# A macaron encoder layer on one core: where tiles start in their partition, once multiples of 32 bytes, now multiples of 512

## Chip, core and metric

The kernel runs on one core of a Trainium2 chip, in one launch. The metric is the device time of an execution in microseconds (us). Engines are named as in the profile: PE is TensorE (PEld its weight loads), DVE VectorE, ACT ScalarE, POOL GpSimd, SP the engine that issues most transfers.

## What is computed

One layer, 512 tokens of 1024 channels, all in float32 (the two SwiGLU blocks have 2816 hidden channels):

```python
h = h + 0.5 * swiglu(rms_norm(h, ffn1_norm), ffn1_w_gate, ffn1_w_up, ffn1_w_down)
u = rms_norm(h, mix_norm) @ w_in            # q 512 | k 128 | v 128 | pool channels 512
a = window_attention(rope(q), rope(k), v, sink_logits)   # +-128 tokens, 8 heads, 2 kv heads
p = multiscale_pool(pc, pool_w, pool_scale)              # windows 2, 4, 8, 16
h = h + concat([a, p]) @ w_out
h = h + 0.5 * swiglu(rms_norm(h, ffn2_norm), ffn2_w_gate, ffn2_w_up, ffn2_w_down)
out = rms_norm(h, final_norm)
```

## The kernel before

Channels lie on the 128 partitions, tokens along the row. Every large product runs in the type float32r, on operands split into a high and a low half (`xh` and `xl` for an activation, `wh` and `wl` for a weight). `mm3` (lines 99 to 102) makes a product of two split operands from three matmuls: high with high, high with low, low with high. Each has a stationary operand of 128 by 128 (`lhsT`) and a moving operand of 128 by 512 (`rhs`). In the names that the profile gives, `ps<-xl,wh` is a product that reads the tiles `xl` and `wh`.

The layer runs in this order, and PE has work nearly throughout:

- `gate_up` of the first SwiGLU. Six output banks are first filled together over the eight channel tiles `k`, then one hidden tile `f` after another. The weights are stationary, `xh` and `xl` move.
- `down` of the first SwiGLU: weights stationary, the hidden values `a1h` and `a1l` move.
- The mixing stage: the input projection moves `yh` and `yl`, which reuse the place of `xh` and `xl`. The scores have queries `qq` stationary and keys `kk`, `kl` moving, 256 or 384 columns wide. The weighted sums move `ph` and `pl`. The output projection moves `pdh`, `pdl` (pool half) and `qq` (attention half, which reuses the queries' place).
- `gate_up` of the second SwiGLU, as the first, with `zh` and `zl` in the place of `xh` and `xl`.
- `down` of the second SwiGLU, the other way round: the hidden values `a2h`, `a2l` are stationary and the weights `wh`, `wl` move. Its last four hidden tiles lie in `late`, which takes the place of `h`, and the last two weight units of its stream are split into `w2`, which takes the place of `xl`.

Weights come in units of 0.75 or 1 MB on SP's queue into `raw`; ACT rounds each half into `wh` (line 88), DVE subtracts to give `wl` (line 89). All tiles come from pools (`base`, `wts`, and one pool for each stage). A pool gives each tile the next free place in the partition, in the order in which the tiles are first named, rounded up to 32 bytes. Small tiles (`warm`, `gain`, `sink`, `psc`, `epsb`, `nst`) stand between the large ones, for instance

```python
    warm = base.tile([P, 1], F32, name="warm")
...
    h = base.tile([P, KD, S], F32, name="h", tag="h")
    gain = base.tile([P, 3, KD], F32, name="gain")
```

Of the kernel before, what the change touches and what calls it, by code (L numbers as in the profile page):

```python
# [8 lines left out]
F32 = mybir.dt.float32  # L9
# [4 lines left out]
P = 128  # L14
D = 1024
S = 512
DFF = 2816
KD = D // P
NF = DFF // P
NT = S // P  # L20
HD = 64
NH = 8
# [8 lines left out]
PAD = 8  # L31
# [3 lines left out]
def encoder_layer(ctx: ExitStack, tc: tile.TileContext, xT, w1h, w1gu, w1d, win, wout, w2h, w2gu, w2d,  # L35
# [3 lines left out]
    base = ctx.enter_context(tc.tile_pool(name="base", bufs=1))  # L39
    wts = ctx.enter_context(tc.tile_pool(name="wts", bufs=2))  # L40
    psp = ctx.enter_context(tc.tile_pool(name="psp", bufs=8, space=bass.MemoryType.PSUM))

    def bank():
        return psp.tile([P, S], F32, name="ps", tag="ps")

# [1 line left out]
    units = [(w1h, i) for i in range(KD // 2)] + [(w1gu, i) for i in range(NF - F0)]  # L47
    units += [(w1d, i) for i in range(NF // 2)] + [(win, i) for i in range(5)]
    units += [(wout, i) for i in range(4)] + [(w2h, i) for i in range(KD // 2)]
# [1 line left out]
    stream = {"asked": 0, "raw": None, "ready": []}  # L51
# [15 lines left out]
        return raw, n  # L67

    def split_next():
        """w = hi + lo, each exact in float32r."""  # L70
        i, half = stream["asked"] // 2, stream["asked"] % 2
        if i == len(units):
            return
        if half == 0 and i:
            stream["raw"] = load(i)
        raw, n = stream["raw"]
        src = raw[:, half * n:(half + 1) * n]
        spare = stream.get("spare")
        if spare:
            wh, wl = spare.pop(0)  # L80
        else:
            wh = wts.tile([P, 1024], F32R, name="wh", tag="wh", bufs=4)[:, :n]
            wl = wts.tile([P, 1024], F32R, name="wl", tag="wl", bufs=4)[:, :n]
        m = n // 2 if stream["asked"] == 0 else n
        on_pool = WIN_POOL if units[i][0] is win else WOUT_POOL if units[i][0] is wout else ()
        sub = nc.gpsimd if 2 * units[i][1] + half in on_pool else nc.vector
        for c in range(0, n, m):
            nc.scalar.copy(wh[:, c:c + m], src[:, c:c + m])  # L88
            sub.tensor_tensor(wl[:, c:c + m], src[:, c:c + m], wh[:, c:c + m].bitcast(F32),  # L89
                              op=ALU.subtract)  # L90
        stream["asked"] += 1
        stream["ready"].append((wh, wl))
# [8 lines left out]
        nc.tensor.matmul(ps, lhsT=ah, rhs=bl, start=False, stop=False)  # L101
        nc.tensor.matmul(ps, lhsT=al, rhs=bh, start=False, stop=stop)  # L102

# [1 line left out]
    ones = base.tile([P, P], F32, name="ones")  # L105
    nc.vector.memset(ones, 1.0)
    warm = base.tile([P, 1], F32, name="warm")
    nc.scalar.copy(warm, ones[:, 0:1])
    ps = bank()
    for i in range(WARM):  # L110
        nc.tensor.matmul(ps[:, 0:P], lhsT=ones, rhs=ones, start=True, stop=True)
    h = base.tile([P, KD, S], F32, name="h", tag="h")
    gain = base.tile([P, 3, KD], F32, name="gain")

    def xload(*ks):
        for k in ks:
# [7 lines left out]
    stream["raw"] = load(0, start)  # L124
    early[1] = load(1)
    xload(4, 5, 6, 7)
    sink = base.tile([P, 1, NH], F32, name="sink")
    nc.gpsimd.dma_start(sink[:, 0, :], sinks)
    psc = base.tile([P, 4], F32, name="psc")
    nc.gpsimd.dma_start(psc, pscale)  # L130
    ident = base.tile([P, P], F32, name="ident")
    make_identity(nc, ident)
    epsb = base.tile([P, 1], F32, name="epsb")
    nc.vector.memset(epsb, EPS)

    acc = base.tile([P, S], F32, name="acc")
# [4 lines left out]
    xl = base.tile([P, KD, S], F32R, name="xl", tag="xl")  # L141

    def norm_in(n, k, xh, xl):
        """gain * h, split; the mean square is gathered beside it."""
        g = gain[:, n, k:k + 1]
        nc.scalar.activation(xh[:, k, :], h[:, k, :], AF.Copy, scale=g)
        nc.vector.scalar_tensor_tensor(xl[:, k, :], h[:, k, :], g, xh[:, k, :].bitcast(F32),  # L147
                                       op0=ALU.mult, op1=ALU.subtract)
        if n == 0:
            if k == 0:  # L150
                nc.gpsimd.tensor_tensor(acc, h[:, k, :], h[:, k, :], op=ALU.mult)
                return
            nc.gpsimd.tensor_tensor(rtmp, h[:, k, :], h[:, k, :], op=ALU.mult)
            nc.gpsimd.tensor_tensor(acc, acc, rtmp, op=ALU.add)
        elif k == 0:
            nc.scalar.activation(acc, h[:, k, :], AF.Square)
        else:
            sq = base.tile([P, S], F32, name="sq", tag="u", bufs=2)
            nc.scalar.activation(sq, h[:, k, :], AF.Square)
            nc.gpsimd.tensor_tensor(acc, acc, sq, op=ALU.add)  # L160

    nst = base.tile([P, 3, NT], F32, name="nst")

    def newton(r, v, b):
        """r = 1 / sqrt(v) from b = sqrt(v), with a step of Newton's."""
        nc.vector.reciprocal(r, b)
        nc.vector.tensor_tensor(b, r, r, op=ALU.mult)
        nc.vector.tensor_tensor(b, b, v, op=ALU.mult)
        nc.vector.tensor_scalar(b, b, -0.5, 1.5, op0=ALU.mult, op1=ALU.add)
        nc.vector.tensor_tensor(r, r, b, op=ALU.mult)  # L170

    def norm_sums():
        """Tokens on partitions: 1 / rms, then a diagonal that the next step spreads."""
        ps = bank()
        for t in range(NT):
            nc.tensor.matmul(ps[:, t:t + 1], lhsT=acc[:, t * P:(t + 1) * P], rhs=ones[:, 0:1],
                             start=True, stop=True)
        r, v, b = (nst[:, j, :] for j in range(3))
        nc.scalar.activation(b, ps[:, 0:NT], AF.Sqrt, scale=1.0 / D, bias=epsb)
        nc.vector.tensor_scalar(v, ps[:, 0:NT], 1.0 / D, EPS, op0=ALU.mult, op1=ALU.add)  # L180
        newton(r, v, b)
        for t in range(NT):
            nc.vector.tensor_scalar(rtmp[:, t * P:(t + 1) * P], ident, r[:, t:t + 1], None, op0=ALU.mult)
        return ps
# [2 lines left out]
        nc.tensor.matmul(ps, lhsT=ones, rhs=rtmp, start=True, stop=True)  # L187
        nc.scalar.copy(rstd, ps)

# [1 line left out]
    def gate_up(xh, xl, act, tmp, after_first, before=None, each=None):  # L191
        def glu(f, pg, pu):
            t1 = tmp.tile([P, S], F32, name="t1", tag="t1", bufs=2)
# [43 lines left out]
                each(f)  # L237

    def down(act, tokens_first, finish):
        """Products over DFF in eight banks; `finish(i, bank)` as each is complete."""  # L240
        banks = [bank() for _ in range(8)]

        def one(i, k, wh, wl, last):
# [21 lines left out]
                one(i, k, wh, wl, k == NF - 1)  # L265
            finish(i, banks[i])

    # ======================= FFN 1 =======================
    with tc.tile_pool(name="ffn1", bufs=1) as fp:
        a1h = fp.tile([P, NF, S], F32R, name="a1h")  # L270
        a1l = fp.tile([P, NF, S], F32R, name="a1l")
# [1 line left out]
                before=lambda k: norm_in(0, k, xh, xl))  # L273
# [6 lines left out]

        down(lambda f: (a1h[:, f, :], a1l[:, f, :]), False, finish1)

    # ======================= mixing =======================
    def weave(main, fill):
        """Runs the steps of `main`, and those of `fill` spread between them."""
        done = 0
        for i, step in enumerate(main):
            step()
            while done < len(fill) and done * len(main) < (i + 1) * len(fill):
                fill[done]()  # L290
                done += 1
        for step in fill[done:]:
            step()

    with tc.tile_pool(name="mix", bufs=1) as mp:
# [1 line left out]
        sr = mp.tile([P, S], F32, name="sr")  # L297
        nc.scalar.dma_start(cr, cosT)
        nc.scalar.dma_start(sr, sinT)
        edge = mp.tile([P, 30], F32, name="edge")  # L300
        nc.scalar.dma_start(edge, edges)
        pw = base.tile([P, 4, P], F32, name="pw", tag="u", bufs=2)
        nc.scalar.dma_start(pw, poolw)
# [7 lines left out]
                                channel_multiplier=-1)  # L311
        nc.gpsimd.affine_select(mask[:, 2, :], mask[:, 2, :], [[-1, P]], ALU.is_ge, NEG, base=0,
                                channel_multiplier=1)
        # Heads of group g keep their values on half g of the partitions, and what a second
        # product needs on the other half: queries [hi; lo], keys [hi; hi] and [lo; 0].
        rows = [slice(0, HD), slice(HD, P)]
        kk = mp.tile([P, 2, S], F32R, name="kk")
        kl = mp.tile([P, 2, S], F32R, name="kl")
# [2 lines left out]
        for t in (kl, vz):  # L321
            nc.gpsimd.memset(t.bitcast(F32), 0.0)
        qq = mp.tile([P, NH, S], F32R, name="qq")
        # a block's queries are dead once its scores are there: its output takes their place
        ath, atl = qq[:, 0:4, :], qq[:, 4:8, :]

        swap = [i + 8 if i < 8 else i - 8 if i < 16 else i for i in range(32)]
# [7 lines left out]
            return u  # L335

        def project(box):
            """The next column tile of the input projection, before the norm's factor."""
            def step(k):
                if k == 0:  # L340
                    box.update(w=weights(), ps=bank())
                c = slice(k * P, (k + 1) * P)
                wh, wl = box["w"]
                mm3(box["ps"], wh[:, c], wl[:, c], yh[:, k, :], yl[:, k, :], k == 0, k == KD - 1)
            return [lambda k=k: step(k) for k in range(KD)]
# [38 lines left out]
        def pool_means(gi, ps):  # L384
            w = POOL_W[gi]
            half = w // 2
            e0 = 2 * (half - 1)
            uu = mp.tile([P, S + 2 * PAD], F32, name="uu", tag="pl", bufs=3)
            n = S + 2 * PAD
            nc.gpsimd.memset(uu[:, :PAD], 0.0)  # L390
            nc.gpsimd.memset(uu[:, n - PAD:], 0.0)
# [28 lines left out]
            steps = []  # L420
# [29 lines left out]
        spread = norm_sums()  # L450
# [106 lines left out]
        ws = {}  # L557

        def project_out(d, bh, bl, finish):
            """Rows of one half of the output projection, for channels of tile d."""  # L560
            def step(i):
                if i == 0:
                    if d % 2 == 0:
# [35 lines left out]
        for d in range(KD):  # L599
            weave(project_out(d, ath, atl, finish_attn), [])  # L600

    # ======================= FFN 2 and the last norm =======================
    with tc.tile_pool(name="ffn2", bufs=1) as fp:
        FB = NF - 4
        a2h = fp.tile([P, FB, S], F32R, name="a2h")
# [66 lines left out]
        down(act2, True, finish2)  # L672


# [1 line left out]
def _arrange(inputs):  # L676
    import numpy as np

# [80 lines left out]
```

## Time and profile before

| | |
|---|---|
| median of 3 runs | 909.97 us (909.09 to 910.32) |
| span of the profiled execution, first to last instruction | 907.0 us |
| the runs' time beyond that span | 2.1 to 3.3 us, 3.0 at the median |
| PE busy | 885.3 us, 98% of the span |
| DVE, ACT, POOL busy | 47%, 34%, 35% |
| mean granted TensorE clock | 0.992 of full |

The time of the profiled execution itself is not listed apart from its span; what lies around the span is taken from the runs. The busy time of PE is the union of its matmuls, each shown longer than the distance to the next, so the rate of PE is read from the distance of starts and not from durations.

### The profile page before, as it was taken

To read this page: it belongs to the slowest core of one execution; us is meant where nothing else is said; L and a number is where in the kernel's file an instruction comes from. 1 tells how busy PE (TensorE), PEld (TensorE's weight loads), DVE (VectorE), ACT (ScalarE), POOL (GpSimd) and SP (SyncE) were. 2 spreads that over 40 slices of the span, in tenths; PEclk is the share of its full clock that TensorE was granted. 3 is DMA by queue.
4 is the path that set the end of the run, shared out by engine and by line. 5 is a ranking of instruction groups with operands and counts; after the bars stand their busy time and mean duration, and the time that the engine had idled before them with its cause. 6 is when DMAs were issued, how large, how long until landed. Compare 5 with 4: busy or idle time off the path is not lost.

```text
span 907.0 us, 9630 instructions
## 1 busy us (share of the span) xinstructions
PE 885.3 (98%) x3882; PEld 718.0 (79%) x3882; DVE 423.4 (47%) x548; ACT 307.1 (34%) x454; POOL 320.5 (35%) x253
## 2 busy tenths in 40 slices
PE   8999999999999999999889999999999999999996
PEld 6778888888888888877668888788888888888885
DVE  7655444444432221659988643444444444322225
ACT  5243223322221221543666532433332222211123
POOL 7375444444420000755542220754334444200004
PEclk9999999999999999999889999999999999999999
DMA  6322222222232322221211123122222222322202
GB/s 233 139 94 94 93 92 93 93 93 92 93 100 112 109 99 93 82 93 46 94 47 36 57 94 116 70 92 93 94 93 93 92 93 93 116 94 103 110 20 93
DMA packets 14796, 84.79 MB, mean 93 GB/s; under 512 B 1952, under 2 KB 2464, under 8 KB 5920
## 3 DMA queue, kind: packets, MB, share of 16 engines
q1 hardware_dynamic: 13392, 81.81, 25.3%
q10 hardware_dynamic: 1296, 2.38, 0.8%
q8 instruction: 30, 0.49, 0.2%
q14 instruction: 14, 0.11, 0.0%
q0 software_dynamic: 64, 0.01, 0.0%
HBM read 82.08 MB, written 2.10 MB: 93 GB/s over the span
## 4 chain that ended last, share of the span: by engine, by line
PE 90%; DVE 7%; issue 1%; ACT 1%; DMA 0%; SPq 0%; DVEq 0%
PE ps L100 29%; PE ps L102 29%; PE ps L101 29%; DVE wl L89 1%; DVE xl L147 1%; DVE qq L365 1%; DVE sc L490 1%; PE ps L523 1%; PE ps L537 1%; DMA h<-in_xT 0%; PE ps L536 0%; PE ps L621 0%; PE ps L488 0%; DVE u L334 0%; DVE rtmp L333 0%
## 5 line engine op out<-in xcount | busy, mean ns | idle before, releaser
L89 DVE TENSOR_TENSOR wl<-raw,wh 128x1024 fp32r<-128x1024 f32 (+2 forms) x146 | 222.8, 1528 | 201.3 <-ACT wh L88 196.5
L88 ACT CAST wh<-raw 128x1024 fp32r<-128x1024 f32 (+2 forms) x153 | 156.7, 1026 | 433.1 <-PE ps L101 349.1
L102 PE MATMUL ps<-xh,wl 128*128 128x512 f32 x346 | 137.4, 397 | 1.8 <-DVE wl L89 1.8
L100 PE MATMUL ps<-zh,wh 128*128 128x512 f32 x346 | 137.6, 398 | 0.0
L101 PE MATMUL ps<-zl,wh 128*128 128x512 f32 x346 | 137.2, 397 | 0.0
L100 PE MATMUL ps<-xh,wh 128*128 128x512 f32 x346 | 136.9, 396 | 0.0
L102 PE MATMUL ps<-zh,wl 128*128 128x512 f32 x346 | 136.9, 396 | 0.0
L101 PE MATMUL ps<-xl,wh 128*128 128x512 f32 x346 | 136.8, 395 | 0.0
L197 POOL TENSOR_TENSOR t<-t,t 128x512 f32<-128x512 f32 x44 | 77.7, 1770 | 150.7 <-ACT t L196 150.7
L199 POOL TENSOR_TENSOR t<-t,rstd 128x512 f32<-128x512 f32 x44 | 60.3, 1374 | 104.9 <-DVE t L198 104.9
L198 DVE TENSOR_TENSOR t<-ps,t 128x512 f32<-128x512 f32 x44 | 30.4, 692 | 125.7 <-PE ps L102 115.0
L102 PEld LDWEIGHTS ps<-xh,wl 128*128 128x128 f32 x346 | 65.0, 188 | 18.4 <-DVE wl L89 2.7
L102 PEld LDWEIGHTS ps<-zh,wl 128*128 128x128 f32 x346 | 65.1, 188 | 15.9 <-issue 0.2
L100 PEld LDWEIGHTS ps<-xh,wh 128*128 128x128 f32 x346 | 65.0, 188 | 15.8 <-issue 0.2
L101 PEld LDWEIGHTS ps<-xl,wh 128*128 128x128 f32 x346 | 65.0, 188 | 15.6
L101 PEld LDWEIGHTS ps<-zl,wh 128*128 128x128 f32 x346 | 65.1, 188 | 15.4 <-issue 0.2
L100 PEld LDWEIGHTS ps<-zh,wh 128*128 128x128 f32 x346 | 65.1, 188 | 15.2
L195 DVE TENSOR_TENSOR t<-ps,rstd 128x512 f32<-128x512 f32 x44 | 30.2, 691 | 97.2 <-PE ps L102 80.7
L100 PE MATMUL ps<-a1h,wh 128*128 128x512 f32 x176 | 68.5, 389 | 0.0
L101 PE MATMUL ps<-a1l,wh 128*128 128x512 f32 x176 | 68.5, 389 | 0.0
L102 PE MATMUL ps<-a1h,wl 128*128 128x512 f32 x176 | 68.5, 389 | 0.0
L89 POOL TENSOR_TENSOR wl<-raw,wh 128x1024 fp32r<-128x1024 f32 x7 | 17.4, 2483 | 114.3 <-ACT wh L88 111.2
(194 smaller groups left out, 1286.5 us busy)
## 6 DMA issues: line engine op xcount, KB each, us to landing
raw<-in_w1gu SPq DMA_DIRECT2D x19, 1024.0 KB, 4.7
raw<-in_w2gu SPq DMA_DIRECT2D x19, 1024.0 KB, 4.7
raw<-in_w1d SPq DMA_DIRECT2D x11, 1024.0 KB, 4.8
raw<-in_w2d SPq DMA_DIRECT2D x11, 1024.0 KB, 4.8
raw<-in_win SPq DMA_DIRECT2D x5, 1024.0 KB, 4.7
raw<-in_wout SPq DMA_DIRECT2D x4, 1024.0 KB, 4.8
raw<-in_w2h SPq DMA_DIRECT2D x4, 768.0 KB, 4.3
raw<-in_w1h SPq DMA_DIRECT2D x3, 768.0 KB, 4.7
```

Source lines behind the costliest of these rows:

```text
L88: nc.scalar.copy(wh[:, c:c + m], src[:, c:c + m])
L89: sub.tensor_tensor(wl[:, c:c + m], src[:, c:c + m], wh[:, c:c + m].bitcast(F32), op=ALU.subtract)
L100: nc.tensor.matmul(ps, lhsT=ah, rhs=bh, start=start, stop=False)
L101: nc.tensor.matmul(ps, lhsT=ah, rhs=bl, start=False, stop=False)
L102: nc.tensor.matmul(ps, lhsT=al, rhs=bh, start=False, stop=stop)
L147: nc.vector.scalar_tensor_tensor(xl[:, k, :], h[:, k, :], g, xh[:, k, :].bitcast(F32), op0=ALU.mult, op1=ALU.subtract)
L195: nc.vector.tensor_tensor(t1, pg, rstd, op=ALU.mult)
L197: nc.gpsimd.tensor_tensor(t2, t2, t1, op=ALU.mult)
L198: nc.vector.tensor_tensor(t1, pu, t2, op=ALU.mult)
L199: nc.gpsimd.tensor_tensor(t1, t1, rstd, op=ALU.mult)
L365: nc.vector.scalar_tensor_tensor(t[o, :], u[r, :], HD ** -0.5, t[r, :].bitcast(F32), op0=ALU.mult, op1=ALU.subtract)
L490: nc.vector.tensor_tensor_reduce(out=sc[:, i, :w], in0=ps[:, :w], in1=mk, scale=1.0, scalar=NEG, op0=ALU.add, op1=ALU.max, accum_out=st[:, ...
```

## The change

The small tiles become slices of one tile `small` of 96 floats (384 bytes), which is named first. Two odd widths are padded: `edge` from 30 to 128 floats, `uu` from 528 to 640 floats; only the old widths are used. Comments are dropped, so line numbers shift by a few.

```diff
+    small = base.tile([P, 96], F32, name="small")
+
+    def cut(a, n):
+        return small[:, a:a + n]
...
-    warm = base.tile([P, 1], F32, name="warm")
+    warm = cut(0, 1)
...
-    gain = base.tile([P, 3, KD], F32, name="gain")
+    gain = cut(8, 24).rearrange("p (n k) -> p n k", n=3)
...
-    sink = base.tile([P, 1, NH], F32, name="sink")
+    sink = cut(32, 8).rearrange("p (n k) -> p n k", n=1)
...
-    psc = base.tile([P, 4], F32, name="psc")
+    psc = cut(40, 4)
...
-    epsb = base.tile([P, 1], F32, name="epsb")
+    epsb = cut(48, 1)
...
-    nst = base.tile([P, 3, NT], F32, name="nst")
+    nst = cut(56, 12).rearrange("p (n k) -> p n k", n=3)
...
-        edge = mp.tile([P, 30], F32, name="edge")
+        edge = mp.tile([P, 128], F32, name="edge")[:, :30]
...
-            uu = mp.tile([P, S + 2 * PAD], F32, name="uu", tag="pl", bufs=3)
+            uu = mp.tile([P, S + 128], F32, name="uu", tag="pl", bufs=3)[:, :S + 2 * PAD]
```

No instruction is added, removed or moved: on every engine the built programs hold the same instructions in the same order, with the same waits and the same semaphore values. What differs is where tiles start. The built programs place them at these bytes, given as the remainder by 512; all slices that a matmul reads are steps of 512 bytes into their tile, so that each operand has the remainder of its tile:

```
tile                                        before         after
xh xl (also yh yl, zh zl, w2)               352            0
wh wl, raw, a1h a1l, a2h a2l                416            0
h (also late)                               160            0
kk kl vv vz qq pdh pdl pwh pwl               32            0
pl (shares its place with uu)               32, 96, 160    0
ph (shares its place with dd)               352            128
sc                                          224            0
acc rstd rtmp                               352            0
ones, ident                                 128, 320       0, 0
```

## Rows read from the trace of the kernel before

**Rows 1.** The page: span, busy time, and PE's granted clock in 40 slices.
```profile
span 907.0 us, 9630 instructions
...
PE 885.3 (98%) x3882; PEld 718.0 (79%) x3882; DVE 423.4 (47%) x548; ACT 307.1 (34%) x454; POOL 320.5 (35%) x253
...
PEclk9999999999999999999889999999999999999999
```

**Rows 2.** PE in order of time, first gate_up, some 10 us: start, duration, instruction.
```profile
100.08 0.39 PE L100 MATMUL ps<-xh,wh 128*128 128x512 f32 x1
100.31 0.40 PE L101 MATMUL ps<-xl,wh 128*128 128x512 f32 x1
...
109.88 0.39 PE L100 MATMUL ps<-xh,wh 128*128 128x512 f32 x1
```

**Rows 3.** The same view, first down, some 10 us.
```profile
299.74 0.39 PE L100 MATMUL ps<-a1h,wh 128*128 128x512 f32 x1
299.97 0.39 PE L101 MATMUL ps<-a1l,wh 128*128 128x512 f32 x1
...
309.94 0.39 PE L100 MATMUL ps<-a1h,wh 128*128 128x512 f32 x1
```

**Rows 4.** The same view, attention half of the output projection.
```profile
509.99 0.40 PE L100 MATMUL ps<-qq,wh 128*128 128x512 f32 x1
...
513.96 0.39 PE L102 MATMUL ps<-qq,wl 128*128 128x512 f32 x1
```

**Rows 5.** The same view, end of the second down: `late` stationary, units alternate.
```profile
877.78 0.39 PE L100 MATMUL ps<-wh,late 128*128 128x512 f32 x1
...
879.14 0.39 PE L100 MATMUL ps<-w,late 128*128 128x512 f32 x1
...
880.54 0.39 PE L100 MATMUL ps<-wh,late 128*128 128x512 f32 x1
...
881.92 0.39 PE L100 MATMUL ps<-w,late 128*128 128x512 f32 x1
```

**Rows 6.** The same view, scores at the lower clock.
```profile
462.31 0.52 PE L488 MATMUL ps<-kk,qq 128*128 128x384 f32 x1
462.63 0.52 PE L489 MATMUL ps<-kl,qq 128*128 128x384 f32 x1
```

**Rows 7.** Groups by line and form: count, busy us, mean ns, idle before.
```profile
L100 PE MATMUL ps<-zh,wh 128*128 128x512 f32 x346 | 137.6, 398 | 0.0
...
L100 PE MATMUL ps<-xh,wh 128*128 128x512 f32 x346 | 136.9, 396 | 0.0
...
L100 PE MATMUL ps<-a1h,wh 128*128 128x512 f32 x176 | 68.5, 389 | 0.0
...
L100 PE MATMUL ps<-wh,a2h 128*128 128x512 f32 x144 | 56.0, 389 | 0.0
...
L100 PE MATMUL ps<-yh,wh 128*128 128x512 f32 x80 | 32.5, 406 | 0.0
...
L100 PE MATMUL ps<-pdh,wh 128*128 128x512 f32 x32 | 13.5, 420 | 0.4 <-ACT pdh L431 0.4
...
L100 PE MATMUL ps<-qq,wh 128*128 128x512 f32 x32 | 12.6, 395 | 0.0
...
L100 PE MATMUL ps<-wh,late 128*128 128x512 f32 x16 | 6.3, 391 | 0.0
```

**Rows 8.** Stretches, all engines: length, busy us (count) of PE, PEld, DVE, ACT, POOL, PEclk, DMA.
```profile
0.00:25.00 25.00, 21.47 (x94) 17.62 (x94) 19.28 (x16) 12.77 (x19) 20.25 (x20) 1.00 0.63 211
...
47.70:256.60 208.90, 208.90 (x896) 168.18 (x895) 93.67 (x80) 65.55 (x82) 98.21 (x64) 1.00 0.26 93
...
376.60:393.00 16.40, 16.40 (x72) 13.16 (x71) 6.54 (x7) 6.42 (x9) 16.24 (x19) 1.00 0.36 113
399.00:428.00 29.00, 28.54 (x124) 22.53 (x123) 28.04 (x38) 12.54 (x18) 16.74 (x16) 1.00 0.11 37
428.00:480.00 52.00, 41.70 (x191) 33.46 (x190) 48.20 (x132) 32.69 (x84) 24.03 (x34) 0.87 0.18 62
480.00:505.70 25.70, 25.70 (x136) 21.30 (x135) 19.72 (x40) 16.11 (x38) 6.11 (x9) 1.00 0.09 32
```

**Rows 9.** The chain that ended last, at its start: start us, us, what.
```profile
22.36 1.78 DVE xl L147
24.14 1.73 DVE wl L89
25.91 0.50 PE ps L102
```

**Rows 10.** Waits, whole span: engine and line, releaser, us in total, times, longest.
```profile
ACT wh L88 <- PE ps L101: 349.1, 108, 4.5
```

**Rows 11.** The chain that ended last: merged rows of the second gate_up's first loop.
```profile
528.35 1.40 PE ps L213 x6
529.74 1.40 PE ps L215 x6
```

## Prediction

> **What bounds the kernel now.** I read the page first. PE is busy for 885.3 of 907.0 us and its clock is at the full level but for two slices [rows 1], while ACT spends 349.1 us waiting for PE to give weight buffers back [rows 10]. So weights and transfers are early, and what counts is the distance from one matmul to the next. That is read in the listing of PE in order of time, where the reader should divide a stretch by its number of matmuls:
>
> - First `gate_up`: from 100.08 to 109.88 us there are 42 steps, 9.80 / 42 = 0.2333 us each [rows 2].
> - First `down`: 299.74 to 309.94, 45 steps, 10.20 / 45 = 0.2267 us each [rows 3].
> - Attention half of the output projection: 509.99 to 513.96, 17 steps, 0.2335 us each [rows 4].
>
> All three are the same work for PE, 512 columns against a 128 by 128 stationary operand, with no wait between. They differ by 6.7 ns. Where does it come from? The table of places says that in `down` moving and stationary operand both start at 416 (by 512), in `gate_up` the moving one at 352 and the stationary one at 416, in the output projection at 32 and 416.
>
> One place separates position from loop order. At the end of the second `down` the same loop, with the same stationary `late` (160), takes its moving operand by turns from `wh` (416) and from `w2` (352). Six matmuls take 1.36 us on `wh` (877.78 to 879.14), then 1.40 us on `w2` (879.14 to 880.54), then 1.38 us on `wh` again [rows 5]. Per matmul that is 0.2267, 0.2333 and 0.2300. So the place of the moving operand alone changes the rate. Loop order doesn't: the first loop of the second `gate_up`, where one moving operand serves six banks in turn, also has 1.40 us for six [rows 11].
>
> **What a column costs at least.** At the lower clock (1.2 GHz, the two slices of the page) a 384-column score product follows the last by 0.32 us [rows 6], which is 384 / 1.2 GHz with nothing on top. At 2.4 GHz, 512 columns alone would be 213.3 ns. The 226.7 ns are 17/16 of that and the 233.3 ns 17.5/16. So every product at the full clock loses something, 13.3 or 20 ns, and nothing at half the clock, as if the reading of four bytes a column just failed to keep up. What the loss would be for an operand at 0 no row shows, since every float32r operand of the kernel before starts 32 bytes past a multiple of 64.
>
> **The change, part by part.** *Instructions.* None is added, removed or moved, and the waits are the same, so the slices of `small` bring no new wait though six tiles are now one. Cost: nothing, with no cover needed.
>
> *Places of DVE, ACT and POOL operands and of the landing places of transfers.* They move too. No row has the same operation at two remainders, so I bound it by what it could touch: these engines and the transfers lie on the end-setting chain in the first 26 us [rows 9] and in 399 to 480 us, where DVE is busy for 28.04 of 29 and 48.20 of 52 us [rows 8]. One per cent of these 107 us is 1 us, either way. I take 0. Elsewhere the 349.1 us of waiting for PE cover it.
>
> *Places of PE's operands.* This is the whole effect. The value at 0 is bounded below by the columns alone, 213.3 ns, and above by the slowest steady rate shown, 233.3 ns (32, the measured remainder nearest to 0, has that). I take 226.7 ns for all products: it is the rate that the trace has where moving and stationary operand share one remainder, which after the change is so everywhere but for the 20 `ph` products, and it lies between the bounds. Then, in matmuls of 512 columns (each is in the count of line 100, 101 or 102, so a count of line 100 stands for three):
>
> 1. `xh`, `zh` products: 346 x 3 each [rows 7], and 36 at the head of the two first loops, 2112. Of these 74 (94 less the 20 warming ones) fall in the first 25 us [rows 8], where the chain runs through DVE until 25.91 [rows 9]; speed there is hidden, the wait for `wl` only grows. 2038 x 6.67 ns = 13.6 us.
> 2. `yh` products: 240 in all [rows 7]. 72 run from 376.6 to 393 us, where PE never idles [rows 8]: 0.5 us.
> 3. From 399 to 480 us PE and DVE set the end by turns: of the 315 entries of PE [rows 8] I take some 180 for products at the full clock, 0 to 1.2 us. DVE's share says that the larger part is covered, PE's that not all is: 0.6 us.
> 4. 480 to 505.7 us: PE never idles (25.70 of 25.70) [rows 8]; of the 32 x 3 `pdh` products [rows 7] some 75 fall here: 0.5 us.
> 5. `qq` products, 32 x 3 [rows 7]: 0.6 us.
> 6. `late`: 48 products on `w2` 0.3 us, and 42 on `wh` at 0.2300, half the difference, 0.1 us.
> 7. `a1h`, `a2h` products, 176 x 3 and 144 x 3 [rows 7], are at 226.7 already: 0.
>
> Sum: 16.3 us. The profiled execution would have a span of 907.0 - 16.3 = 890.7; with the 3.0 us that the median run has beyond the span, 893.7 us. Nothing else becomes the bound: `gate_up` gives one hidden tile 48 x 0.2267 = 10.9 us, and from 47.7 to 256.6 us POOL, the next, is busy for 98.21 of 208.90 us [rows 8]. What is late next is still PE.
>
> **What a page of the notes says.** The Trainium skill, "SBUF — State Buffer", section Specifications, has lines of 16 bytes, with a penalty for each access that goes to a new line and full speed for two or more hits per line. Every operand before starts at a multiple of 32 and runs on without steps, so by it there is nothing to gain and the time stays at 910. The trace doesn't agree: at multiples of 16 alike, the rates differ by 6.7 ns [rows 5]. The same skill, "TensorE: Matmul & The Clock Gate", section "Wait — 56ns, not 53.3ns?", gives 215.7 ns from start to start for 512 columns at the full clock. No row of this kernel is that fast; by it the time would be an estimated 856 us.
>
> **Rivals.**
>
> *Faster still: at 0 the loss goes away.* For it: the loss scales with the columns (17/16), as a reading that straddles something in every stretch of 64 bytes would make it, and all operands before have the odd 32 bytes. Against: no row shows a rate below 226.7. At 213.3 ns the faster class (1008 products: terms 6 and 7) gains 13.3 ns each, 13.4 us, and the slower class (some 2440 that are not hidden) 20 ns, 48.8 us: 907.0 - 62.2 + 3.0 = 848. At 220, halfway, it is 6.7 and 32.5 us: 871. Its centre is some 860.
>
> *No change: the place is not what decides.* For it: the three measured stages differ in more than remainders, and remainders by 512 may not be the ones that matter, so that 0 could happen to give each stage what it has. Against: [rows 5] and [rows 11]. 910.
>
> *Slower: 0 behaves like 32.* If the moving operand's own place decides and low remainders are bad, 416 was the lucky one: all go at 233.3, the 1008 fast products lose 6.7 ns, 6.7 us: 916.7. For it: 32 is nearest to 0, and the first six products on `wh` run at 226.7 though `late` is at 160, so that sharing a remainder is not needed. Against: 352 has the same loss as 32, so that low or high is not the rule. It decides from the point where 2440 x (233.3 - c) = 1008 x (c - 226.7), c = 231.4 ns.
>
> *In between:* a rate of 229 to 231 ns, as after the turn back to `wh` in [rows 5]: at 230 the slower class gains 8.1 us and the faster loses 3.3, 905.
>
> **How the numbers follow.** Chances: 226.7 everywhere 0.40; faster still 0.32; in between 0.07; no change 0.12; slower 0.09. The predicted time is that of the first, 893.7 (891 to 897 for itself, by terms 3 and the 1 us of the other engines). A measurement of this kernel tells about 0.2% from no change (1.8 us). Faster by more: 0.40 + 0.32 + 0.07 = 0.79; within: 0.12; slower: 0.09. For 8 in 10 the range goes from 853, which leaves out only the extreme of the faster rival, to 910, which takes in half of no change.
>
> **What would show it.** In the trace after, the distance of starts in the first `gate_up`, in `down` and in the output projection: 226.7 in all three for my forecast, below 222 for the faster rival, 233.3 in `down` for the slower one, unchanged for none. At the end of the second `down` units should no longer take turns. The first 26 us and 399 to 480 us should keep their length within 1 us. I am wrong if the rate at 0 is not 226.7, above all since no row has an operand there, or if DVE or ACT change their durations with the place.

## The result and the profile after

The kernel after takes 894.86 us (892.55 to 895.28, 4 runs), the kernel before 909.76 us (909.09 to 910.32, 4 runs): ratio 0.9829, 95% interval 0.9811 to 0.9847. It is faster by 14.9 us; 893.7 was predicted.

The page of the kernel after shows the same number of instructions in a span 14.0 us shorter than [rows 1], and PE as the bound:

```profile
span 893.0 us, 9630 instructions
...
PE 869.3 (97%) x3882; PEld 717.4 (80%) x3882; DVE 422.3 (47%) x548; ACT 306.7 (34%) x454; POOL 320.1 (36%) x253
```

PE in order of time, kernel after (start, duration, instruction): the first `gate_up`, the first `down`, the attention half of the output projection, and the end of the second `down`, as in [rows 2 to 5].

```profile
100.01 0.39 PE L106 MATMUL ps<-xh,wh 128*128 128x512 f32 x1
...
109.98 0.39 PE L108 MATMUL ps<-xh,wl 128*128 128x512 f32 x1
...
299.70 0.39 PE L108 MATMUL ps<-a1h,wl 128*128 128x512 f32 x1
...
309.90 0.39 PE L108 MATMUL ps<-a1h,wl 128*128 128x512 f32 x1
...
509.01 0.39 PE L106 MATMUL ps<-qq,wh 128*128 128x512 f32 x1
...
512.86 0.39 PE L108 MATMUL ps<-qq,wl 128*128 128x512 f32 x1
...
866.97 0.39 PE L106 MATMUL ps<-wh,late 128*128 128x512 f32 x1
...
868.33 0.39 PE L106 MATMUL ps<-w,late 128*128 128x512 f32 x1
...
869.69 0.39 PE L106 MATMUL ps<-wh,late 128*128 128x512 f32 x1
```

The reader divides again. `gate_up`: 9.97 us for 44 steps, 226.6 ns where it was 233.3. `down`: 10.20 us for 45, 226.7 as before. Output projection: 3.85 us for 17, 226.5 where it was 233.5. At the end six matmuls take 1.36 us on `wh` and 1.36 us on `w2`; they no longer take turns. So one rate holds in all four stretches, and the time came from the stages that had 233.3. It does not hold yet for the pool half of the output projection, whose products run in threes between other ones (see point 4 of the account below). ACT still waits mostly for PE, in the waits of the kernel after (engine and line, releaser, us, times, longest):

```profile
ACT wh L94 <- PE ps L107: 333.8, 108, 4.4
```

### The profile page after: what moved, and what is told of

Read it like the earlier page. It is cut to its first block, busy times and chain, and to the rows that moved or that the text cites. A ratio compares the mean times of both kernels' runs of the same rounds, so it can differ in the third digit from the quotient of the medians.

```text
span 893.0 us, 9630 instructions
## 1 busy us (share of the span) xinstructions
PE 869.3 (97%) x3882; PEld 717.4 (80%) x3882; DVE 422.3 (47%) x548; ACT 306.7 (34%) x454; POOL 320.1 (36%) x253
## 4 chain that ended last, share of the span: by engine, by line
PE 90%; DVE 6%; ACT 2%; issue 1%; DMA 0%; SPq 0%; DVEq 0%; ACTq 0%
PE ps L106 29%; PE ps L108 29%; PE ps L107 29%; DVE wl L95 1%; ACT sc L507 1%; DVE qq L371 1%; DVE xl L153 1%; PE ps L529 1%; PE ps L543 1%; DMA h<-in_xT 0%; PE ps L542 0%; DVE sc L496 0%; PE ps L627 0%; PE ps L494 0%; DVE u L340 0%
## 5 line engine op out<-in xcount | busy, mean ns | idle before, releaser
L108 PE MATMUL ps<-xh,wl 128*128 128x512 f32 x346 | 135.3, 391 | 3.3 <-DVE wl L95 3.3
L106 PE MATMUL ps<-zh,wh 128*128 128x512 f32 x346 | 135.5, 392 | 0.0
L107 PE MATMUL ps<-zl,wh 128*128 128x512 f32 x346 | 135.1, 390 | 0.0
L108 PE MATMUL ps<-zh,wl 128*128 128x512 f32 x346 | 134.8, 390 | 0.0
L106 PE MATMUL ps<-xh,wh 128*128 128x512 f32 x346 | 134.8, 389 | 0.0
L107 PE MATMUL ps<-xl,wh 128*128 128x512 f32 x346 | 134.6, 389 | 0.0
L106 PEld LDWEIGHTS ps<-zh,wh 128*128 128x128 f32 x346 | 65.0, 188 | 13.3
L95 POOL TENSOR_TENSOR wl<-raw,wh 128x1024 fp32r<-128x1024 f32 x7 | 17.3, 2469 | 114.3 <-ACT wh L94 111.3
```

The source lines that it names most:

```text
L106: nc.tensor.matmul(ps, lhsT=ah, rhs=bh, start=start, stop=False)
```

## The experiments

Theory A says that the relation of the moving to the stationary operand decides; theory B that the moving operand's own place does. Remainders are by 512 unless said otherwise.

**1. Everything at 352.** The kernel after, moved up as a whole, so that all operands share a slow place of before:

```diff
-    small = base.tile([P, 96], F32, name="small")
+    small = base.tile([P, 184], F32, name="small")
```

> The kernel after with everything moved up by 352 bytes, so that moving and stationary operands all start at 352 (by 512), the place at which the moving operands of gate_up stood before. Theory A (the relation of moving and stationary operand decides; one shared remainder gives 226.7 ns a product): 226.7 ns in every stage, time as after, 895 us within 2. Theory B (the moving operand's own place decides, and 352 is a slow one, 0 and 416 fast ones): 233.3 ns in every stage, some 3450 products 6.7 ns slower, 23 us: 918 us.

Measured 896.29 us, ratio to before 0.9846 (0.9823 to 0.9870). PE in the first `gate_up` of this kernel, 44 steps in 9.97 us, 226.6 ns:

```profile
99.89 0.39 PE L108 MATMUL ps<-xh,wl 128*128 128x512 f32 x1
...
109.86 0.39 PE L107 MATMUL ps<-xl,wh 128*128 128x512 f32 x1
```

Theory B falls: 352 is no slow place by itself. That 0 is a multiple of 64 or 512 gives nothing either, since 352 is as good.

**2. One part alone.** The kernel before, with 64 bytes of padding ahead of `xh` and `xl`, and nothing else of the change:

```diff
+    base.tile([P, 16], F32, name="pad0")
     xh = base.tile([P, KD, S], F32R, name="xh", tag="xh")
     xl = base.tile([P, KD, S], F32R, name="xl", tag="xl")
+    base.tile([P, 112], F32, name="pad1")
```

> The kernel before with one part of the change alone: 64 bytes of padding ahead of xh and xl (and 448 behind, so that the large tiles behind stay), so that the moving operands of both gate_up stages and of the input projection start at 416 like their weights. Theories A and B both: 226.7 ns in gate_up instead of 233.3, the output projection stays at 233.3; the gain is nearly that of the whole change, 13 to 14 of the 15 us: 896 us. If the gain of the change came from the padding of small operands or from the other engines' operands: 910 us.

Measured 895.78 us, ratio 0.9850 (0.9830 to 0.9870). PE in the first `gate_up`, 44 steps in 9.98 us, 226.8 ns:

```profile
99.93 0.39 PE L102 MATMUL ps<-xh,wl 128*128 128x512 f32 x1
...
109.91 0.39 PE L101 MATMUL ps<-xl,wh 128*128 128x512 f32 x1
```

The output projection, whose operands are left at 32 and 416, stays slow, 18 steps in 4.20 us, 233.3 ns:

```profile
508.75 0.39 PE L100 MATMUL ps<-qq,wh 128*128 128x512 f32 x1
...
512.95 0.39 PE L100 MATMUL ps<-qq,wh 128*128 128x512 f32 x1
```

Two paddings give nearly the whole gain. `small` and the padding of `edge` and `uu` aren't needed for it.

**3. The weights alone moved away.** The kernel after, with `raw`, `wh`, `wl` at 64 and all else at 0:

```diff
+    fill = ctx.enter_context(tc.tile_pool(name="fill", bufs=1))
...
+    wts.tile([P, 16], F32, name="pad0", bufs=1)
+    fill.tile([P, 112], F32, name="pad1")
```

> The kernel after with raw, wh and wl alone moved up by 64 bytes. In gate_up, the first down and the projections the stationary operand goes to 64 and the moving one stays at 0; in the second down it is the other way round. Theory A: 230 to 233.3 ns in all of these, 3.3 to 6.7 ns on 3450 products, 906 to 918 us. Theory B: gate_up and the first down stay at 226.7, only the second down can change; 895 to 898 us.

Measured 916.57 us, ratio to before 1.0079 (1.0061 to 1.0097): slower than the kernel before. PE in the first `gate_up` (10.27 us for 44 steps), the first `down` (6.07 us for 26) and the second `down` (6.07 us for 26), 233.4 to 233.5 ns in all three:

```profile
99.67 0.40 PE L110 MATMUL ps<-xl,wh 128*128 128x512 f32 x1
...
109.94 0.40 PE L109 MATMUL ps<-xh,wh 128*128 128x512 f32 x1
...
299.87 0.40 PE L110 MATMUL ps<-a1l,wh 128*128 128x512 f32 x1
...
305.94 0.40 PE L109 MATMUL ps<-a1h,wh 128*128 128x512 f32 x1
...
819.75 0.40 PE L110 MATMUL ps<-wl,a2h 128*128 128x512 f32 x1
...
825.82 0.40 PE L109 MATMUL ps<-wh,a2h 128*128 128x512 f32 x1
```

64 bytes between the two operands cost 21.7 us against the kernel after (916.57 to 894.86), in the `down` stages too, which were fast before. Theory A stands in the kernel itself.

**4. Trains.** The kernel after, and behind its last product trains of 24 matmuls (8 products in float32) with nothing beside them. Each takes its operands from `w2` (moving) and `a2h` (stationary), both at 0 in this kernel, moved by `mv` and `st` bytes:

```diff
+        def tries(mv, st, n=512, dt=None, count=24):
+            ps = bank()
+            for j in range(count):
+                m0 = j % 3 * 1024 + mv // 4
+                x = w2[:, m0:m0 + n]
+                y = a2h[:, j % 8, st // 4:st // 4 + P]
...
+                nc.tensor.matmul(ps[:, :n], lhsT=y, rhs=x, start=j == 0, stop=j == count - 1)
```

> The kernel after, and behind its last product 45 trains of 8 or 24 matmuls that are not part of the reference, with nothing else running: float32r with the moving operand at 16 remainders and the stationary at 0, the stationary at 8 remainders and the moving at 0, equal and unequal pairs of before, 384 and 256 columns, two trains in bfloat16, two in float32. Its time is not comparable; the steps of the trains are. Theory A: 226.7 ns at every equal pair, 230 to 233.3 at the others, by the difference alone. Theory B: the step follows the moving operand's remainder alone. Both: bfloat16, half the bytes a column, at 214 to 217 ns whatever the place, if what is lost is lost in reading four bytes a column; 226 or 233 there too if it is not.

A row here merges matmuls that follow each other: the stretch less the last one's duration, by the count less one, is the step. A pair like 128/0 means moving operand at 128, stationary at 0. In this order: moving 0 and stationary 0; 128 and 0; the end of 0 and 256; 256 columns at 0 and 0; and bfloat16 at 352 and 416.

```profile
904.89 4.92 PE L700 MATMUL ps<-w,a2h 128*128 128x512 f32 x21
...
932.61 5.06 PE L700 MATMUL ps<-w,a2h 128*128 128x512 f32 x21
...
1023.82 3.11 PE L700 MATMUL ps<-w,a2h 128*128 128x512 f32 x13
...
1100.34 1.48 PE L700 MATMUL ps<-w,a2h 128*128 128x256 f32 x11
...
1116.68 4.05 PE L700 MATMUL ps<-acc,rtmp 128*128 128x512 bf16 x18
```

(4.92 - 0.39) / 20 = 226.5 ns; (5.06 - 0.39) / 20 = 233.5; (3.11 - 0.39) / 12 = 226.7; (1.48 - 0.28) / 10 = 120; (4.05 - 0.39) / 17 = 215. From the starts of the single records, the mean step of the last twelve of each train:

```
moving - stationary, by 256      512 columns, float32r, ns
0    (0/0, 32/32, 64/64, 352/352, 416/416, 256/0, 0/256, 416/160)   226.7
+64  (64/0, 320/0)                                                  228.9
+16  (16/0)                                                         231.7
+32, +96, +192, +224 (at 0 to 480 over 0), -16, -32, -64            233.3
+128 (128/0, 384/0; 0/128, 32/416)                                  233.3; 232.5, 232.6
+160 (160/0, 416/0)                                                 234.3, 233.8
                                 other widths and types
384 columns 0/0, 32/0, 64/0, 352/416                                173.3, 173.3, 173.3, 174.6
256 columns 0/0, 32/0, 64/0, 352/416                                120.0, 117.8, 117.8, 117.8
bfloat16, 512 columns, 0/0, 352/416                                 215.8, 215.8
float32 (a product is two such matmuls), 0/0, 352/416               429.1, 429.3
```

Theory A holds, and more sharply than it was put: what must agree is the remainder by 256, not by 512. Equal by 256 gives 226.7 ns wherever the pair stands. What an unequal pair costs is not settled by the difference alone. In the trains 64 bytes ahead cost 2.2 ns and 64 behind 6.7; but the second `down` of experiment 3 has its moving operand (64) ahead of its stationary one (0) by 64 too, and takes 233.5 ns (the last two rows shown there). Differences of 128 give 233.3 or 232.5 to 232.6. Why is open. bfloat16 and float32 don't care about the place in the two pairs tried. And what is lost at an equal place is 13.3 ns for 256, 384 and 512 columns alike (120.0, 173.3 and 226.7 against 106.7, 160 and 213.3 of the columns alone at 2.4 GHz), so it is not a sixteenth of the columns.

**5. Equal by 256, and at no multiple of 64.** The kernel of the second run, with `edge` padded too, which puts the tiles of the mixing stage at 160 beside weights at 416:

```diff
-        edge = mp.tile([P, 30], F32, name="edge")
+        edge = mp.tile([P, 62], F32, name="edge")[:, :30]
```

> The kernel before with x moved by 64 bytes as in the second run, and edge padded by 128 bytes, so that the tiles of the mixing stage start at 160; large operands then lie at 160 or 416, equal by 256 but not by 512, and none at a multiple of 64. Theory A as the trains have it (the difference by 256 decides, nothing else): 226.7 ns in every stage, the output projection too, 895 us as the kernel after. If multiples of 512 or of 64 matter by themselves: output projection stays at 233.3, 896 to 897 us.

Measured 895.31 us, ratio 0.9832 (0.9807 to 0.9857), that of the whole change. PE in the output projection, moving 160 and stationary 416, 18 steps in 4.08 us, 226.7 ns:

```profile
510.79 0.39 PE L100 MATMUL ps<-qq,wh 128*128 128x512 f32 x1
...
514.87 0.39 PE L100 MATMUL ps<-qq,wh 128*128 128x512 f32 x1
```

**6. What the last 13.3 ns are: more trains,** with 32 to 128 stationary columns (`m`), and with other pairs.

```diff
-                y = a2h[:, j % 8, st // 4:st // 4 + P]
+                y = a2h[:, 0 if still else j % 8, st // 4:st // 4 + m]
```

> The kernel after and 23 trains behind its last product, which are not part of the reference; the time is not comparable. Theory C (the 13.3 ns that stay at an equal place are lost to the load of the next stationary operand, which reads beside the moving one): with 32, 64 and 96 stationary columns 3.3, 6.7 and 10 ns are lost, 216.7, 220 and 223.3 ns at equal places. Theory D (a loss of the moving read itself, 17/16): 226.7 ns whatever the number of stationary columns. Pairs that differ by +64: 228.9 at any absolute place if the difference alone counts; 4 and 8 bytes apart: between 226.7 and 233.3; the same stationary operand again and again: as with changing ones, since each matmul loads it.

Both theories fall. At equal places 32, 64 and 96 stationary columns give 231.7, 230.0 and 230.0 ns: fewer columns cost more, not less. With 384 moving columns it makes no difference: 173.3 ns with 32, 64, 96 and 128 stationary columns. A row of the 32-column train, (4.10 - 0.39) / 16 = 231.9:

```profile
952.61 4.10 PE L698 MATMUL ps<-w,a2h 128*32 128x512 f32 x17
```

The pairs do what the difference says in the trains before: +64 at 128/64, 192/128, 96/32 and 0/192 all give 228.8 to 228.9; 128/384 and 160/416 give 226.6 to 226.7. Four bytes apart give 236.7, eight 233.3. The same stationary operand again and again gives 226.7, as a changing one (233.3 at 128/0, again as a changing one).

**7 and 8. Both kernels profiled once more,** for the first 28 us.

> The kernel before, profiled once more, for the first 28 us: the profile shown has its 100th entry of PE at 27.41 us, that of after and of four other kernels at 28.6 to 29.0. If that is one execution's luck, it comes at 28.5 or more here; if the kernel before starts faster, at 27.4 again.

> The kernel after, profiled once more, beside the run before it: the 100th entry of PE near 28.6 us, the gate_up stages at 226.7 ns, a span of 893 to 895 us.

The 100th entry of PE (entries are counted from 0, here and below) is at 29.01 us in the kernel before and at 28.21 in the kernel after, the other way round than in the first pair (27.41 and 28.57). So the head start of the first profile of before was that execution's luck. The first `gate_up` of the kernel after is at 226.7 ns again. The spans are 909.0 and 891.7 us; the second is shorter than the 893 to 895 expected.

**9. By turns, one column, other widths.** Trains that take a float32r and a bfloat16 matmul by turns, trains with 1, 16 and 112 stationary columns, and 320 and 448 moving columns:

```diff
+                if j % 2:
+                    x, y = b16[0][:, mv // 2:mv // 2 + S], b16[1][:, st // 2:st // 2 + P]
+                else:
+                    x, y = w2[:, m0:m0 + S], a2h[:, j % 8, st // 4:st // 4 + P]
```

> The kernel after and trains behind its last product, which are not part of the reference; the time is not comparable. What is left at an equal place is 13.3 ns over the columns alone, the same for 256, 384 and 512 columns, and it does not fall with 32 to 96 stationary columns. Theory C2 (it is lost where a float32r moving operand is read while a float32r stationary operand is loaded): in trains that take float32r and bfloat16 matmuls by turns each step is at 214 to 217 ns, also with the places 128 bytes apart, since the one or the other reads two bytes a column; with 1 stationary column nearly nothing is lost, 214 to 217; 320 and 448 columns at equal places 146.7 and 200 ns. Theory E (each float32r matmul has its own fixed cost of 13.3 ns): by turns 226.7 for the float32r step and 215.8 for the bfloat16 step; 1 column 226.7.

Neither theory holds. By turns, the records of a float32r matmul start 0.46 us apart, 230 ns on average for each of the pair, at both pairs of places; that is more than C2's 214 to 217 and more than E's mean of 221. In the train (start, duration):

```profile
951.24 0.58 PE L718 MATMUL ps<-w,a2h 128*128 128x512 f32 x1
951.67 0.39 PE L718 MATMUL ps<-acc,rtmp 128*128 128x512 bf16 x1
951.70 0.58 PE L718 MATMUL ps<-w,a2h 128*128 128x512 f32 x1
```

One and 16 stationary columns give 231.7 ns, 112 give 228.9. 320 columns take 146.7 ns at an equal place, 13.3 over the columns alone; 448 take 206.7, which is 20 over, and 203.3 with the operands 128 bytes apart, so at 448 columns, as at 256, the equal place is the slower one. At 320 the two places take the same 146.7. The fixed 13.3 ns is thus no rule for every width, and neither is the gain of equal places.

## Why the prediction was right

1. *PE's step is the bound.* Right. With the same instructions and waits the time went down with the step alone, and experiment 3 brought it up again by nothing but a place.
2. *The value at 0: 226.7 ns for all products, because both operands share a remainder.* Right, in value and in the reason (experiments 1 to 5). It was a choice: no row of before had an operand at 0, and the prediction gave it a chance of 0.40, with 0.32 for the faster rival. It was put too narrowly: by 256 is enough. That settles what the prediction held against itself, the six products on `wh` at 226.7 with `late` at 160: 416 and 160 are equal by 256. The 1.38 us after each turn back from `w2` fits a settling: in the trains too the first three to some ten matmuls after a change to an equal pair keep an uneven, slower step.
3. *The sum of 16.3 us.* Nearly right. From the 100th entry of PE to the end, the part on which the sum stands, the two profiles of before take 879.6 and 880.0 us, the two of after 864.4 and 863.5: 15.2 to 16.5 us. The 768 steps from the 300th to the 1068th entry went from 179.20 to 174.08 us, 6.67 ns each; the attention half of the output projection (95 steps) from 22.17 to 21.53; the last 81 steps from 18.77 to 18.36. The spans of the first pair differ by 14.0 only, since before started 1.2 us earlier there; those of the second pair by 17.3.
4. *399 to 505 us.* I gave 0.6 us to term 3 and 0.5 to term 4, and term 4 was too large. From the 2026th entry (480 us in the kernel before) to the first `qq` product the first pair takes 25.70 and 25.59 us, the second 25.69 and 25.60: 0.1 us less. Most products there run in threes between those of the attention. The steps from one `pdh` or `pdl` product to the next (55, leaving out ten of over 310 ns in either kernel) average 231.6 ns before and 230.8 after, though all their operands start at 0. That fits the settling of point 2, which takes three matmuls and more, but was not tested apart; only the unbroken run at the end comes from 230.0 ns (six steps in 1.38 us) to 226.7 (six in 1.36):

```profile
496.75 0.40 PE L106 MATMUL ps<-pdh,wh 128*128 128x512 f32 x1
...
498.13 0.39 PE L106 MATMUL ps<-pdh,wh 128*128 128x512 f32 x1
...
499.49 0.39 PE L106 MATMUL ps<-qq,wh 128*128 128x512 f32 x1
```

From the 1700th to the 2100th entry, 390 to 490 us, the first pair gains 0.5 us and the second 1.8. Two executions of one kernel differ there by 0.4 us (before) and 0.9 (after), so term 3 can't be told from this scatter. DVE still sets much of it, in these stretches of the kernel after (length, busy us and count of PE, PEld, DVE, ACT, POOL, PEclk, DMA; compare [rows 8]):

```profile
398.00:421.00 23.00, 21.97 (x99) 17.86 (x98) 22.88 (x29) 9.71 (x15) 16.39 (x16) 1.00 0.12 46
421.00:473.00 52.00, 41.33 (x192) 33.19 (x191) 48.47 (x132) 33.01 (x84) 24.05 (x34) 0.87 0.16 62
```

5. *Other engines' operands and landing places: nothing.* DVE is busy for 422.3 us after 423.4, ACT for 306.7 after 307.1, POOL for 320.1 after 320.5: no change that counts.
6. *The rivals.* "Faster still" rested on the reading that the loss scales with the columns, as if an odd 32 bytes caused it. Both are refuted: at 0 there are the same 226.7 ns as at 352, and 256 and 384 columns lose the same 13.3 ns. My rate as "17/16 of the columns" was right for 512 columns alone. "Slower" and "no change" are refuted by the result, and theory B, on which the first stood, by experiment 1. The line rule of the Trainium skill, "SBUF — State Buffer", section Specifications (TRN2), from which the prediction took it that 16-byte multiples are all alike, doesn't cover this: 64 bytes between the operands cost 21.7 us in experiment 3. The 215.7 ns of the Trainium skill, "TensorE: Matmul & The Clock Gate", section "Wait — 56ns, not 53.3ns?", are there in the bfloat16 trains (215.8) and in no float32r train.

What stays open is what the last 13.3 ns are. They aren't taken by the number of stationary columns, nor by the moving read alone, and mixing types doesn't remove them. That the two reads of PE get in each other's way, which a rule of equal remainders by 256 suggests, was only argued. Open is also what sets the step at unequal places, since the trains and the kernel of experiment 3 differ at the same 64 bytes.

## What to carry to other kernels

Where float32r products of 512 columns bound a kernel, divide a stretch of PE's starts by its matmuls, stage by stage; if the same width shows two rates, compare where moving and stationary operand start, and bring their remainders by 256 together. Other widths need their own measurement: at 256 and 448 columns equal places were the slower ones, by 2.2 and 3.4 ns. And the rate wants a run of such products: where they stood in threes between others, the gain was 0.8 ns each and not 6.7. Two paddings of a pool do it, here for 1.5% of the time, and one small tile in the wrong place can undo it and more (2.4% in experiment 3). Multiples of 512 are a convenient way, not the cause; bfloat16 and float32 products showed no such dependence in the pairs tried.

## What the runs showed of the hardware

- The step of a 512-column float32r matmul at the full clock lies between 226.7 and 236.7 ns by where its operands start. With equal remainders by 256 it is 226.7 at every place tried; else 233.3 at most differences and 236.7 at 4 bytes. With the moving operand 64 ahead it was 228.9 in trains and 233.5 in a kernel.
- After a change to an equal pair, or after other matmuls in between, the step took three to some ten matmuls to settle at 226.7 ns.
- At 256 and 448 columns equal places are not the best: 120.0 ns against 117.8, and 206.7 against 203.3.
- A narrower stationary operand made the train slower: 231.7 ns with 1, 16 or 32 columns, 226.7 with 128. At 384 moving columns it made none of this difference, 173.3 ns with 32 to 128.
- float32r and bfloat16 by turns take 230 ns each on average, though bfloat16 alone takes 215.8 and float32r alone 226.7.
